# A hybrid attention and mLSTM layer on one core: the mLSTM heads' norm weight applied in ScalarE's copies, and a new order of the three products of a matmul

## The chip, the core and the metric

The kernel runs on one core of one Trainium2 chip. The core has a matrix engine (TensorE, PE in the profile, with its weight loads listed apart as PEld), a vector engine (VectorE, DVE), a scalar engine (ScalarE, ACT), a general engine (GpSimd, POOL) and a queue engine (SyncE, SP) that here only issues DMAs. Each engine runs its own instructions in order; they meet through semaphores. The metric is the device time of one execution in microseconds. Three runs of the kernel before took 2602.81, 2605.07 and 2609.3 us: median 2605.07 us.

## What is computed

One layer of a diffusion backbone over 256 latent tokens and 256 context tokens of width 2048, all in fp32: a half-step SwiGLU feed-forward, a mixer of eight attention heads and eight bidirectional mLSTM heads, and a second feed-forward (latent tokens alone). The change is in the mixer's end and in how every fp32 product is made. Of the reference:

```python
def mixer_output(att, hm, mo, m_gain, w_out):
    B, T = att.shape[:2]
    hm = rms_norm(hm, m_gain.reshape(M_HEADS, HEAD_DIM)) * mo.reshape(B, T, M_HEADS, HEAD_DIM)
    return jnp.concatenate([att.reshape(B, T, ATT_Q_W), hm.reshape(B, T, M_W)], axis=-1) @ w_out
```

`hm` are the mLSTM heads' outputs, `mo` is the sigmoid of a projection, and `m_gain` is the norm's weight: one number for each of the 8 x 128 channels of the heads, the same for all tokens. So it may be multiplied in at any point between the norm and the product with `w_out`.

## The kernel before

**Products in three parts.** An fp32 operand is held as a high part `hi` (rounded to the matrix engine's fp32r type) and a low part `lo`, the rest. A product of two such operands is three matmuls into the same PSUM bank: high by high, high by low and low by high. `mm3` (L147 to L151) makes them. Its arguments are the output, the stationary operand's two parts `sh`, `sl` and the moving operand's two parts `mh`, `ml`. Before, L149 is `sh` by `mh`, L150 is `sh` by `ml`, L151 is `sl` by `mh`. In a profile row of a matmul the name behind the arrow is the moving operand, then the stationary one: `mm<-hi,hhi` moves a weight's high part past an activation's high part.

In most calls the activations stand still and the weights move. In three places the weights stand still: the fourth up-projection tile of both feed-forwards (L764, L1963) and `channels` (L1437), which projects the mLSTM queries and keys.

**Weights.** `load_split` (L140) has SP load a tile of 128 x 2048 fp32 into one of three `raw` buffers. `split` (L119) then makes, for each half of 1024 columns, the high part by a ScalarE copy (L127) and the low part by a VectorE subtraction (L128), each into a ring of four buffers. So the high part of a half is always done first, its low part a copy's and a subtraction's time later; a buffer is free again when the last matmul that reads it is done. The Strassen-like stages of the feed-forwards (`quad`, `pair`) take part of their weights from `chain` and `ra` buffers, to which GpSimd's queue adds further weights by accumulating DMAs (L730). Beside all this, VectorE makes the modulation vectors by long multiply-and-sum instructions (L207), whose rows SP loads (`sraw`, `sr`, `late`).

**The mixer's end.** The heads' outputs lie in `hm`, tokens on partitions. `ev_o` (L1625) evacuates the projection `mo`: a sigmoid on ScalarE into `gm` (L1627), and then a GpSimd product of `gm` with `mg` (L1628), the norm weight broadcast over all partitions by a DMA of SP (L1673). `mlstm_out` (L1719) squares and sums the heads (L1725, L1727), has GpSimd make the reciprocal root (L156, L157), and multiplies `hm` on VectorE by `gm` (L1729) and by the root (L1730). `mlstm_cat` (L1735) turns `hm` with four 128 x 128 transposes into a PSUM bank, channels on partitions, and ScalarE copies the bank to `cx` (L1743), 128 x 512 in one instruction. There are four such copies (two groups of heads, two token tiles). `mlstm_split` then splits `cx` into the `cathi`, `catlo` operand of the output projection `out_proj` (L1804).

In the same stretch runs `attention` (L1676), in steps woven between the projections' matmuls: three products to the scores, the row maximum and its scaling on VectorE (L1686, L1687), the exponential on ScalarE (L1690), the reciprocal sum and a scaling on VectorE (L1691, L1692), transposes on TensorE (L1698), a ScalarE copy (L1700), and the product with the values (L1707).

**What sets the order.** The source gives the order of work by generators that are stepped by hand (`weave`, `steps`). From it the program's builder lays out each engine's instructions, by times it assumes for them; only pinned instructions keep the source's order. So an instruction that costs another time, or depends on another one, can shift others on its engine.

Of the kernel before, what the change touches and what calls it, by code (L numbers as in the profile page):

```python
# [9 lines left out]
F32 = mybir.dt.float32  # L10
# [3 lines left out]
AF = mybir.ActivationFunctionType  # L14
ALU = mybir.AluOpType
# [4 lines left out]
P = 128  # L20
D = 2048
KT = D // P
T = 256
HD = 128
NH = 8
# [33 lines left out]
def tile_layer(ctx: ExitStack, tc: tile.TileContext, I: dict, out: bass.AP):  # L59
    nc = tc.nc  # L60
    pool = lambda **k: tc.tile_pool(**k)

    cst = ctx.enter_context(pool(name="cst", bufs=1))
# [29 lines left out]
    vector, tensor, scalar = [nc.vector], [nc.tensor], [nc.scalar]  # L93
# [12 lines left out]
    triangle(ident, ones, 1)  # L106
    triangle(ident, ident, -1)

    vecs = cst.tile([P, 9 * KT + 3 * KT + 16 * 5 + 16], F32, name="vecs")
    bmT = vecs[:, 0:144].rearrange("p (c k) -> p c k", c=9)  # L110
    gnT = vecs[:, 144:192].rearrange("p (c k) -> p c k", c=3)
    cwT = vecs[:, 192:272].rearrange("p (m j) -> p m j", j=5)
    cbT = vecs[:, 272:288]

    def raw_tile(n=2048):
        t = wp.tile([P, 2048], F32, tag="raw", name="raw", bufs=3)
# [27 lines left out]
        next(beside["load"], None)  # L144
        return wt

    def mm3(out_ap, sh, sl, mh, ml, first, last, skip=False):  # L147

        tensor[0].matmul(out_ap, sh, mh, start=first, stop=False, skip_group_check=skip)  # L149
        tensor[0].matmul(out_ap, sh, ml, start=False, stop=False, skip_group_check=skip)  # L150
        tensor[0].matmul(out_ap, sl, mh, start=False, stop=last, skip_group_check=skip)  # L151

    def rsqrt_mean(ss, n, width=1):

# [35 lines left out]
    nc.scalar.activation(cc, cc, AF.Silu)  # L190
    SC = cst.tile([P, 3, 2, KT], F32, name="SC")
    SH = cst.tile([P, 3, 2, KT], F32, name="SH")
    cst.tile([P, 48], F32, name="cstpad")
    mod_rows = {i: dr.tile([2, D], F32, name=f"mod{i}") for i in (2, 5, 8)}
    mT = cst.tile([P, 9, 2, KT, 2], F32, name="mT")

# [69 lines left out]
    class Beside:  # L266
# [26 lines left out]
        def one(self):  # L293
            i, kt, h = self.items[self.n]
            x, limit = self.slots[self.n]
            mod_half(x, {LAT: self.cB}, None, i, (LAT,), kt, h)
            self.due.append((self.done + 1, self.n))
            self.n += 1
# [158 lines left out]
    hhi = hpool.tile([P, KT, 512], F32R, tag="hh", name="hhi")  # L457
    hlo = hpool.tile([P, KT, 512], F32R, tag="hl", name="hlo")

    pre = [[bank(), bank()] for _ in range(NPRE)]  # L460
    with pool(name="st", bufs=1) as st:
# [61 lines left out]
        rest = []  # L523
# [102 lines left out]
        for n, (s, t) in enumerate(((CTX, 1), (LAT, 0), (LAT, 1))):  # L626
# [5 lines left out]
            last, r = r, factor(ss)  # L632
# [14 lines left out]
        for k0, k1 in BLOCKS[1:]:  # L647
# [26 lines left out]
            if k1 - k0 == 1:  # L674
                tb = tbank()
# [55 lines left out]
    with pool(name="f1u", bufs=1) as f1u:  # L731
# [26 lines left out]
        for f in range(NPRE, FB):  # L758
            pab = []
            for ab in range(2):  # L760
                wt = load_split(I["w_up1"][f - NPRE, ab])
                b = bank()
                for k in range(KT):
                    mm3(b, *wt(slice(k * P, (k + 1) * P)), hhi[:, k, :], hlo[:, k, :], k == 0, k == KT - 1)  # L764
                pab.append(b)
            tail(f, pab)

# [405 lines left out]
    hhi = hpool.tile([P, KT, 512], F32R, tag="hh", name="hhi")  # L1173
    hlo = hpool.tile([P, KT, 512], F32R, tag="hl", name="hlo")
# [79 lines left out]
    with ExitStack() as mx:  # L1254
# [144 lines left out]
        C1 = one([P, NH, 2, 130], "C1")  # L1399
# [32 lines left out]
        def channels(name, h, N, b):  # L1432

            wt = load_split(I[name][h])
            for k in range(KT):
                w = slice(k * P, (k + 1) * P)
                mm3(b, *wt(w), hhi[:, k, 512 - N :], hlo[:, k, 512 - N :], k == 0, k == KT - 1)  # L1437
                if k % 4 == 3:
                    next(beside["part"], None)
                    yield  # L1440
# [11 lines left out]
        for h in range(NH):  # L1452
            b = bank()
# [171 lines left out]
        def ev_o(c, t, b):  # L1625
            o = gm[:, t - 2, c * 512 : (c + 1) * 512]
            nc.scalar.activation(o, b, AF.Sigmoid)  # L1627
            nc.gpsimd.tensor_tensor(o, o, mg[:, c * 512 : (c + 1) * 512], op=ALU.mult)  # L1628

        av = one([P, 4, 256], "av", tag="slot0")  # L1630

# [37 lines left out]
            nc.scalar.activation(k1[:, x], keys[1][x].bitcast(F32), AF.Copy)  # L1669
        keys[1] = [k1[:, x] for x in range(2)]  # L1670
        gm = one([P, 2, 1024], "gm", tag="mkT")
        mg = one([P, 1024], "mg", tag="C1")
        nc.sync.dma_start(mg, I["m_gain"].partition_broadcast(P))  # L1673
        catf = one([P, NH, T], "catf", tag="v1l")

        def attention(kv):  # L1676
# [56 lines left out]
        cxs = {}  # L1733

        def mlstm_cat(c):  # L1735

            for t in range(2):
                tb = tbank()
                for g in range(4):
                    o = (4 * c + g) * P  # L1740
                    nc.tensor.transpose(tb[:, g * P : (g + 1) * P], hm[:, t, o : o + P], ident)
                cxs[c, t] = m1.tile([P, 512], F32, tag="nM", name="cx")
                nc.scalar.activation(cxs[c, t], tb, AF.Copy)  # L1743
                yield

        bo = ({}, {})
# [181 lines left out]
    with f2x:  # L1928
# [28 lines left out]
        for f in range(NPRE, FB):  # L1957
            pab = []
            for ab in range(2):
                wt = load_split(I["w_up2"][f - NPRE, ab])  # L1960
                b = (tbank() if f == FB - 1 else bank())[:, :T]
                for k in range(KT):
                    mm3(b, *wt(slice(k * P, (k + 1) * P)), h2hi[:, k, :T], h2lo[:, k, :T], k == 0, k == KT - 1)  # L1963
                pab.append(b)
            sa = sab_tile()[:, :T]
            nc.scalar.activation(sa, pab[0], AF.Silu)
            gated = nc.vector.tensor_tensor(sa, sa, pab[1], op=ALU.mult)
            split_hid(hids[0], f, sa)
# [379 lines left out]
def _laid_out(a):  # L2348
    asc = np.ascontiguousarray
    part = lambda v: v.reshape(-1, P).T  # L2350
    m = {
        "x": asc(a["x"][0]),
        "ctx": asc(a["ctx"][0]),
        "cc": asc(np.concatenate([a["c_ctx"].reshape(KT, P), a["c"].reshape(KT, P)])),
        "b_mod": asc(a["b_mod"][0].reshape(9, D)),
        "gate_b": asc(a["gate_b"][0]),
        "m_gain": asc(a["m_gain"][0]),
        "q_gain": asc(a["q_gain"][0]),
        "k_gain": asc(a["k_gain"][0]),
        "g_final": asc(a["g_final"]),  # L2360
        "rope": _rope_tables(),
    }
    cw = a["conv_w"][0].T.reshape(16, P, 5).transpose(1, 0, 2).reshape(P, 80)
    m["vecs"] = asc(np.concatenate([part(a["b_mod"][0]), part(a["g_norm"][0]), cw, part(a["conv_b"][0])], 1))

    wm = a["w_mod"][0].reshape(D, 9, D)

    def units(i, a_, b):
        n = (b - a_) * P
        k = 2048 // n  # L2370
        return wm[:, i, a_ * P : b * P].reshape(KT // k, k, P, n).transpose(0, 2, 1, 3).reshape(KT // k, P, 2048)

    def block(k0, k1):

        still = [wm[:, 0, k0 * P : (k0 + 1) * P].T[None]] if k1 - k0 == 2 else []
        return still + [units(0, k1 - 1, k1), units(1, k0, k1)]

    m["w_m0"] = asc(np.concatenate([u for b in BLOCKS for u in block(*b)]))
    m["w_mt"] = asc(wm[:, 2:].reshape(D, 7, KT, P).transpose(1, 2, 3, 0))
    for n in "12":  # L2380
        up, dn = a[f"w_ffn{n}_up"][0], a[f"w_ffn{n}_down"][0]
        nf = dn.shape[0] // P
        up = up.reshape(KT, P, 2, nf, P)

        rest = up[:, :, :, FB:].reshape(4, 4, P, 2, nf // FB - 1, CB)
        m[f"w_up{n}b"] = asc(rest.transpose(4, 3, 0, 2, 1, 5).reshape(nf // FB - 1, 2, 4, P, 2048))
        first = up[:, :, :, :FB].transpose(3, 2, 1, 0, 4).reshape(-1, 2, P, 2048)
        m[f"w_up{n}"] = asc(first[NPRE:])
        pre = first[:NPRE].reshape(2 * NPRE, P, KT, P)
        loads = []  # L2390
        for k0, k1 in BLOCKS if n == "1" else BLOCKS2:
            most = min(2 * NPRE, 2048 // ((k1 - k0) * P) // 2 * 2)
            loads += [pre[u : u + most, :, k0:k1].transpose(1, 0, 2, 3).ravel() for u in range(0, 2 * NPRE, most)]
        m[f"w_pre{n}"] = asc(np.concatenate(loads))
        m[f"w_dn{n}"] = asc(dn.reshape(NF // FB, FB, P, NCB, CB).transpose(0, 3, 2, 1, 4).reshape(NF // FB, NCB, P, 2048))
    w = a["w_in"][0]

    def tokens_still(cols):
        n = cols.shape[1]
        return asc(cols.reshape(4, 4, P, n).transpose(0, 2, 1, 3).reshape(4, P, 4 * n))  # L2400

    def tokens_move(c0):
        return asc(w[:, c0 : c0 + 1024].reshape(KT, P, NH, P).transpose(2, 1, 0, 3).reshape(NH, P, 2048))

    m["w_a"] = tokens_still(np.concatenate([w[:, GT0:], w[:, MV0 : MV0 + 384]], 1))
    m["w_b"] = tokens_still(w[:, MV0 + 384 : MV0 + 768])
    m["w_c"] = asc(w[:, MV0 + 768 : MV0 + 1024].reshape(2, 8, P, 256).transpose(0, 2, 1, 3).reshape(2, P, 2048))
    m["w_mk"], m["w_mq"] = tokens_move(MK0), tokens_move(MQ0)
    m["w_kv"] = tokens_still(w[:, AK0 : AK0 + 512])
    for c in range(2):  # L2410
        m[f"w_q{c}"] = tokens_still(w[:, AQ0 + 512 * c : AQ0 + 512 * (c + 1)])
        m[f"w_o{c}"] = tokens_still(w[:, MO0 + 512 * c : MO0 + 512 * (c + 1)])
    m["w_out"] = asc(a["w_out"][0].reshape(4, 4, P, NCB, CB).transpose(3, 0, 2, 1, 4).reshape(NCB, 4, P, 2048))
    return m
# [15 lines left out]
```

## Time and profile before

| | |
|---|---|
| median of three runs | 2605.07 us |
| profiled execution, its own time | 2604.58 us |
| its span, first to last instruction | 2602.7 us |
| mean granted TensorE clock | 0.996 |
| VectorE busy | 2170.6 us (83%) |
| ScalarE busy | 1417.7 us (54%) |
| GpSimd busy | 220.7 us (8%) |

The profile is one execution: the page sums up engines, queues and the costliest groups of instructions; other views list instructions in order of time, who waited for whom, and the busy time of each engine in a given stretch. A row of an instruction in order of time has its start, its duration (both us), its engine and line, and in brackets how long its engine had been idle and what released it. Matmul durations overlap: a matmul starts before the one before it has drained, so what counts is the distance from start to start. By stage: the first 130 us are the start-up, the first feed-forward lasts to about 1340 us, the mixer to about 1900 us, the second feed-forward to the end.

### The profile page before, as it was taken

Reading aid. Unit: us, or ns where it says so; the run is one execution under the profiler, and the core shown is the slowest. Engines: PE = TensorE matmul, PEld = TensorE weight load, DVE = VectorE, ACT = ScalarE, POOL = GpSimd, SP = SyncE. Lnnn points to the kernel's source line nnn. Section 1 sums busy time; section 2 is a strip of 40 time slices with the busy share of each in tenths; the row PEclk is TensorE's granted clock in tenths of the full one; section 3 lists DMA queues with packets and bytes.
Section 4 is the critical chain, followed back from the end, with each engine's and each line's share of the span. In section 5 each row is a group of like instructions: output and inputs, shape, how many; then the busy total and the mean of one; then the engine's idle time right before and its main releaser. Section 6 shows DMA issues by size and latency. Waiting matters only on the chain.

```text
span 2602.7 us, 33781 instructions
## 1 busy us (share of the span) xinstructions
PE 2575.7 (99%) x12670; PEld 2144.7 (82%) x12670; DVE 2170.6 (83%) x2864; ACT 1417.7 (54%) x1810; POOL 220.7 (8%) x269
## 2 busy tenths in 40 slices
PE   8999999999999999999999999999999999999998
PEld 5788888888888888888889889888897888888887
DVE  7788888878888788888887889798889878887887
ACT  4454444544444565444454347456476676666664
POOL 0000000100000100000110000120000000000001
PEclk8999999999999999999999999999999999999999
DMA  9889999999999988889987887776768988999876
GB/s 392 350 217 265 276 277 271 262 273 285 261 287 265 278 247 240 218 215 228 225 253 266 296 312 247 242 273 213 267 239 240 269 269 260 272 273 279 256 231 176
DMA packets 127219, 681.01 MB, mean 262 GB/s; under 512 B 14152, under 2 KB 16712, under 8 KB 64976
## 3 DMA queue, kind: packets, MB, share of 16 engines
q1 hardware_dynamic: 98544, 493.25, 50.7%
q0 software_dynamic: 28512, 185.61, 36.4%
q8 instruction: 99, 1.62, 0.2%
q14 instruction: 64, 0.52, 0.1%
HBM read 660.91 MB, written 17.89 MB: 261 GB/s over the span
## 4 chain that ended last, share of the span: by engine, by line
PE 85%; DVE 7%; DMA 5%; issue 2%; ACT 1%; POOL 0%; ACTq 0%; POOLq 0%; SPq 0%; DVEq 0%
PE mm L151 21%; PE mm L150 21%; PE mm L149 21%; DVE lo L128 2%; PE mm L87 2%; PE Y L149 2%; PE Y L151 2%; PE Y L150 2%; PE X L151 2%; PE X L150 2%; PE X L149 2%; PE tr L150 1%; PE tr L149 1%; PE tr L151 1%; PE tr L87 1%
## 5 line engine op out<-in xcount | busy, mean ns | idle before, releaser
L127 ACT ACTIVATE hi<-raw 128x1024 fp32r<-128x1024 f32 (+2 forms) x500 | 517.8, 1041 | 421.1 <-PE mm L151 264.1
L128 DVE TENSOR_TENSOR lo<-raw,hi 128x1024 fp32r<-128x1024 f32 (+2 forms) x488 | 583.6, 1207 | 149.7 <-ACT hi L127 130.5
L127 ACT ACTIVATE hi<-chain 128x1024 fp32r<-128x1024 f32 x336 | 355.0, 1059 | 305.7 <-PE mm L151 188.0
L128 DVE TENSOR_TENSOR lo<-chain,hi 128x1024 fp32r<-128x1024 f32 x336 | 407.2, 1221 | 118.0 <-ACT hi L127 114.3
L149 PE MATMUL mm<-hi,hhi 128*128 128x512 f32 (+3 forms) x1024 | 393.6, 385 | 0.0
L151 PE MATMUL mm<-hi,hlo 128*128 128x512 f32 (+3 forms) x1024 | 386.7, 378 | 0.0
L150 PE MATMUL mm<-lo,hhi 128*128 128x512 f32 (+3 forms) x1024 | 386.7, 378 | 0.0
L207 DVE SCALAR_TENSOR_TENSOR junk<-sraw,cBh 128x1024 fp8e5<-128x1024 f32 x192 | 234.3, 1220 | 19.2 <-DMA sraw<-in_w_mt 16.7
L151 PEld LDWEIGHTS mm<-hi,hlo 128*128 128x128 f32 x1024 | 192.5, 188 | 33.9
L149 PEld LDWEIGHTS mm<-hi,hhi 128*128 128x128 f32 x1024 | 192.6, 188 | 31.0
L150 PEld LDWEIGHTS mm<-lo,hhi 128*128 128x128 f32 x1024 | 192.8, 188 | 30.7
L128 DVE TENSOR_TENSOR lo<-ra,hi 128x1024 fp32r<-128x1024 f32 x96 | 117.0, 1223 | 39.7 <-ACT hi L127 35.8
L127 ACT ACTIVATE hi<-ra 128x1024 fp32r<-128x1024 f32 x96 | 101.9, 1061 | 65.1 <-PE mm L151 48.4
L149 PE MATMUL mm<-hi,hid2h 128*128 128x512 f32 x352 | 137.1, 390 | 0.0
L151 PE MATMUL mm<-hi,hid2l 128*128 128x512 f32 x352 | 137.0, 389 | 0.0
L150 PE MATMUL mm<-lo,hid2h 128*128 128x512 f32 x352 | 136.9, 389 | 0.0
L207 DVE SCALAR_TENSOR_TENSOR sr<-sr,cBl 128x1024 f32<-128x1024 f32 x84 | 103.0, 1234 | 14.7 <-DMA sr<-in_w_mt 13.8
L730 POOL DMA_DIRECT2D chain<-in_w_up1b x60 | 53.1, 886 | 726.0 <-DVE lo L128 648.9
L149 PE MATMUL mm<-hhi,hi 128*128 128x512 f32 (+1 forms) x288 | 101.4, 352 | 0.0
L151 PE MATMUL mm<-hhi,lo 128*128 128x512 f32 (+1 forms) x288 | 99.0, 344 | 0.0
L150 PE MATMUL mm<-hlo,hi 128*128 128x512 f32 (+1 forms) x288 | 98.7, 343 | 0.0
L149 PE MATMUL mm<-hi,sumshl 128*128 128x512 f32 x200 | 77.8, 389 | 0.0
(517 smaller groups left out, 5650.3 us busy)
## 6 DMA issues: line engine op xcount, KB each, us to landing
raw<-in_w_dn SPq DMA_DIRECT2D x70, 1024.0 KB, 7.5
chain<-in_w_up1b POOLq DMA_DIRECT2D x60, 1024.0 KB, 9.8
sraw<-in_w_mt SPq DMA_DIRECT2D x96, 512.0 KB, 7.8
sr<-in_w_mt SPq DMA_DIRECT2D x81, 512.0 KB, 5.5
raw<-in_w_up1b SPq DMA_DIRECT2D x40, 1024.0 KB, 7.9
mraw<-in_w_m SPq DMA_DIRECT2D x32, 1024.0 KB, 7.4
raw<-in_w_up2b SPq DMA_DIRECT2D x32, 1024.0 KB, 9.9
chain<-in_w_dn POOLq DMA_DIRECT2D x30, 1024.0 KB, 8.6
```

Of the source, the lines that this page charges most:

```text
L87: ins = getattr(self.engine, name)(*a, **k)
L127: scalar[0].activation(hi, src, AF.Copy)
L128: vector[0].tensor_tensor(lo, src, hi.bitcast(F32), op=ALU.subtract)
L149: tensor[0].matmul(out_ap, sh, mh, start=first, stop=False, skip_group_check=skip)
L150: tensor[0].matmul(out_ap, sh, ml, start=False, stop=False, skip_group_check=skip)
L151: tensor[0].matmul(out_ap, sl, mh, start=False, stop=last, skip_group_check=skip)
L207: ins = nc.vector.scalar_tensor_tensor(junk() if junk else raw, raw, 1.0, cB[s], op0=ALU.mult, op1=ALU.mult, accum_out=mT[:, i, s, kt, h : ...
L730: accum = lambda dst, src: nc.gpsimd.dma_start(dst, src, accum_op=ALU.add)
```

## The change

Three parts.

1. `vecs`, the tile of small vectors loaded at the start, grows by 8 columns, `mgT`, which hold the norm weight with channels on partitions. A pad (`cstpad`) shrinks by 8 columns, so that what lies behind it stays where it was. The load of `mg` and its tile are gone.
2. The four GpSimd products with `mg` are gone. The four ScalarE copies of 128 x 512 to `cx` become sixteen copies of 128 x 128, one for each head and token tile, each with that head's column of `mgT` as its scale for each partition.
3. `mm3` now makes `sh` by `mh`, then `sl` by `mh`, then `sh` by `ml`. Calls where the weights stand still pass `still=True` and keep the old order, so that in every call with weights the weights' low part is read last.

```diff
-    vecs = cst.tile([P, 9 * KT + 3 * KT + 16 * 5 + 16], F32, name="vecs")
+    vecs = cst.tile([P, 9 * KT + 3 * KT + 16 * 5 + 16 + NH], F32, name="vecs")
+    mgT = vecs[:, 288:296]
...
-    def mm3(out_ap, sh, sl, mh, ml, first, last, skip=False):
-
-        tensor[0].matmul(out_ap, sh, mh, start=first, stop=False, skip_group_check=skip)
-        tensor[0].matmul(out_ap, sh, ml, start=False, stop=False, skip_group_check=skip)
-        tensor[0].matmul(out_ap, sl, mh, start=False, stop=last, skip_group_check=skip)
+    def mm3(out_ap, sh, sl, mh, ml, first, last, skip=False, still=False):
+
+        rest = ((sh, ml), (sl, mh)) if still else ((sl, mh), (sh, ml))
+        for n, (s, m) in enumerate(((sh, mh), *rest)):
+            tensor[0].matmul(out_ap, s, m, start=first and not n, stop=last and n == 2, skip_group_check=skip)
...
-    cst.tile([P, 48], F32, name="cstpad")
+    cst.tile([P, 40], F32, name="cstpad")
...
             nc.scalar.activation(o, b, AF.Sigmoid)
-            nc.gpsimd.tensor_tensor(o, o, mg[:, c * 512 : (c + 1) * 512], op=ALU.mult)
...
-        mg = one([P, 1024], "mg", tag="C1")
-        nc.sync.dma_start(mg, I["m_gain"].partition_broadcast(P))
...
-                nc.scalar.activation(cxs[c, t], tb, AF.Copy)
+                for g in range(4):
+                    w = slice(g * P, (g + 1) * P)
+                    nc.scalar.activation(cxs[c, t][:, w], tb[:, w], AF.Copy, scale=mgT[:, 4 * c + g : 4 * c + g + 1])
```

The calls at L764, L1437 and L1963 get `still=True`, and the host's layout of the inputs puts the norm weight into `vecs`.

More of the change, by code (lines that the diff above doesn't have):

```diff
@@ L763, in tile_layer @@
                 for k in range(KT):
-                    mm3(b, *wt(slice(k * P, (k + 1) * P)), hhi[:, k, :], hlo[:, k, :], k == 0, k == KT - 1)
+                    mm3(b, *wt(slice(k * P, (k + 1) * P)), hhi[:, k, :], hlo[:, k, :], k == 0, k == KT - 1, still=True)
                 pab.append(b)
@@ L1436, in channels @@
                 w = slice(k * P, (k + 1) * P)
-                mm3(b, *wt(w), hhi[:, k, 512 - N :], hlo[:, k, 512 - N :], k == 0, k == KT - 1)
+                mm3(b, *wt(w), hhi[:, k, 512 - N :], hlo[:, k, 512 - N :], k == 0, k == KT - 1, still=True)
                 if k % 4 == 3:
@@ L1962, in tile_layer @@
                 for k in range(KT):
-                    mm3(b, *wt(slice(k * P, (k + 1) * P)), h2hi[:, k, :T], h2lo[:, k, :T], k == 0, k == KT - 1)
+                    mm3(b, *wt(slice(k * P, (k + 1) * P)), h2hi[:, k, :T], h2lo[:, k, :T], k == 0, k == KT - 1, still=True)
                 pab.append(b)
@@ L2356, in _laid_out @@
         "gate_b": asc(a["gate_b"][0]),
-        "m_gain": asc(a["m_gain"][0]),
         "q_gain": asc(a["q_gain"][0]),
@@ L2363, in _laid_out @@
     cw = a["conv_w"][0].T.reshape(16, P, 5).transpose(1, 0, 2).reshape(P, 80)
-    m["vecs"] = asc(np.concatenate([part(a["b_mod"][0]), part(a["g_norm"][0]), cw, part(a["conv_b"][0])], 1))
+    m["vecs"] = asc(np.concatenate([part(a["b_mod"][0]), part(a["g_norm"][0]), cw, part(a["conv_b"][0]), part(a["m_gain"][0])], 1))
     wm = a["w_mod"][0].reshape(D, 9, D)
```

## The prediction

> **What bounds the kernel now.** I read the page's shares first, then the chain of waits, then the wait list of TensorE, then stretches of the time line. The page:
>
> ```profile
> span 2602.7 us, 33781 instructions
> PE 2575.7 (99%) x12670; PEld 2144.7 (82%) x12670; DVE 2170.6 (83%) x2864; ACT 1417.7 (54%) x1810; POOL 220.7 (8%) x269
> PE 85%; DVE 7%; DMA 5%; issue 2%; ACT 1%; POOL 0%; ACTq 0%; POOLq 0%; SPq 0%; DVEq 0%
> PE mm L151 21%; PE mm L150 21%; PE mm L149 21%; DVE lo L128 2%; PE mm L87 2%; PE Y L149 2%; PE Y L151 2%; PE Y L150 2%; PE X L151 2%; PE X L150 2%; PE X L149 2%; PE tr L150 1%; PE tr L149 1%; PE tr L151 1%; PE tr L87 1%
> ```
>
> TensorE is busy all but 27 us of the span, and the three lines of `mm3` are the chain. So a gain has to come either from the distance at which matmuls follow each other, or from TensorE's idle time. The idle time by stretch (stretch, its length, then busy us of PE, PEld, DVE, ACT and POOL with their instructions):
>
> ```profile
> 0.00:130.00 130.00, 120.08 (x961) 82.54 (x962) 97.69 (x185) 58.55 (x116) 4.18 (x13) 0.95 0.93 371
> 130.00:1480.00 1350.00, 1348.43 (x6231) 1130.36 (x6230) 1124.21 (x1412) 666.66 (x777) 125.76 (x150) 1.00 0.92 256
> 1480.00:1680.00 200.00, 199.32 (x1118) 173.84 (x1117) 170.61 (x327) 112.95 (x214) 12.92 (x18) 1.00 0.79 273
> 1680.00:1840.00 160.00, 156.10 (x825) 130.30 (x824) 139.99 (x261) 93.80 (x148) 26.35 (x26) 1.00 0.72 249
> 2500.00:2602.70 102.70, 93.36 (x419) 76.85 (x418) 76.62 (x93) 47.11 (x58) 8.08 (x10) 0.97 0.66 201
> ```
>
> Start-up idles 9.9 us; its products are not made by `mm3`. The last stretch idles 9.3 us, nearly all behind the last matmul. What lies between is 27.0 - 9.9 - 9.3 = 7.8 us, and 3.9 of it falls into 1680 to 1840 us, where the heads' norm weight is applied. All that the change can win by ending waits is these 7.8 us.
>
> **Part 1, the order of the products.** What TensorE waited for, and what the makers of the parts waited for (who, for whom: us in total, times, longest):
>
> ```profile
> ACT hi L127 <- PE mm L151: 500.6, 408, 5.3
> DVE lo L128 <- ACT hi L127: 280.7, 250, 4.3
> PE Y L150 <- DVE lo L128: 0.3, 1, 0.3
> PE mm L150 <- DVE lo L128: 0.3, 1, 0.3
> ```
>
> TensorE waits 0.6 us in all for a low part that moves (L150). The new order asks for that part one product later, so at most 0.6 us goes; the makers wait for TensorE and not the reverse. The other side: where the *activation's* low part is the late one, the new order asks for it a product earlier. That is so at the first products of the output projection:
>
> ```profile
> 1791.53 0.45 PE L149 MATMUL mm<-hi,cathi 128*128 128x512 f32 x1
> 1791.82 0.39 PE L150 MATMUL mm<-lo,cathi 128*128 128x512 f32 x1
> 1791.96 0.19 PEld L151 LDWEIGHTS mm<-hi,catlo 128*128 128x128 f32 x1 [0.18 <-DVE catlo L1800]
> ```
>
> L150 of this group now stands behind the wait for `catlo`: so the wait hides one product less: 0.29 us from L149's start to L150's, for each of two token tiles, 0 to +0.6 us; I take +0.3. Against that I take -0.3 of the 0.6. Part 1 sums to 0, between -0.6 and +0.6.
>
> That leaves the matmuls' distance. In the middle of the first feed-forward:
>
> ```profile
> 600.39 0.39 PE L149 MATMUL mm<-hi,s2h 128*128 128x512 f32 x1
> 600.62 0.39 PE L150 MATMUL mm<-lo,s2h 128*128 128x512 f32 x1
> 600.85 0.39 PE L151 MATMUL mm<-hi,s2l 128*128 128x512 f32 x1
> 601.08 0.39 PE L149 MATMUL mm<-hi,s2h 128*128 128x512 f32 x1
> ...
> L150 PEld LDWEIGHTS mm<-lo,hhi 128*128 128x128 f32 x1024 | 192.8, 188 | 30.7
> L151 PEld LDWEIGHTS mm<-hi,hlo 128*128 128x128 f32 x1024 | 192.5, 188 | 33.9
> ```
>
> Each starts 0.23 us after the one before, whether the stationary part is the same as before (L149 to L150) or another. A weight load of 188 ns runs under every matmul: 12670 loads for 12670 matmuls on the page. So giving up the shared stationary part costs nothing. The Trainium skill's page "TensorE: Matmul & The Clock Gate" (section "Step-by-step: what each phase is for") speaks against the change: loading is a separate instruction so that one can load once and multiply repeatedly, and the new order never uses a stationary part twice in a row. By that rule the change adds a load to each group, and is slower; by the rows no load is saved before, so none is added. It is a rival below.
>
> **Part 2, the GpSimd products.** In the mixer's end, in order of time:
>
> ```profile
> 1728.95 2.13 POOL L1628 TENSOR_TENSOR gm<-gm,mg 128x512 f32<-128x512 f32 x1
> 1729.85 2.31 DVE L207 SCALAR_TENSOR_TENSOR sr<-sr,cBl 128x1024 f32<-128x1024 f32 x1
> 1735.62 1.30 POOL L1628 TENSOR_TENSOR gm<-gm,mg 128x512 f32<-128x512 f32 x1
> 1736.95 0.69 DVE L1729 TENSOR_TENSOR hm<-hm,gm 128x512 f32<-128x512 f32 x1 [2.38 <-POOL gm L1628]
> 1740.32 0.39 PE L151 MATMUL mm<-hhi,hlo 128*128 128x512 f32 x1
> 1743.23 0.68 DVE L1686 TENSOR_REDUCE nm<-mm 128x1 f32<-128x512 f32 x1
> 1743.83 1.21 DVE L207 SCALAR_TENSOR_TENSOR sr<-sr,cBl 128x1024 f32<-128x1024 f32 x1
> 1747.50 0.49 DVE L1692 TENSOR_SCALAR pr<-pr,sd 128x512 f32<-128x512 f32 x1
> 1748.13 0.63 PE L1698 MATMUL tr<-ident,pr 128*128 128x128 f32 x4 [2.14 <-DVE pr L1692]
> 1760.60 0.69 DVE L1729 TENSOR_TENSOR hm<-hm,gm 128x512 f32<-128x512 f32 x1 [2.61 <-POOL gm L1628]
> ```
>
> VectorE idles 2.38 us for a GpSimd product, and one of its long instructions takes 2.31 us beside the other product against 1.21 a little later: 3.5 us lost before 1737 us. The scores of an attention step are there at 1740.32 + 0.39 = 1740.7, but VectorE reaches their maximum only at 1743.23, 2.5 us late, with earlier work in front. From there the step runs to `pr` at 1747.50, and TensorE stands 2.14 us at its transposes. Without the products `hm` by `gm` waits for the sigmoid alone, VectorE is 3.5 us ahead, the maximum starts when the scores are there, and the 2.5 us saved cover the 2.14. So -2.1 us. Bounds: 0, if other work of VectorE fills the time, and -3.9, all the idle time of the stretch. I take -2.1, the row that names the wait. The second wait, of 2.61, freed too, has no stall of TensorE behind it. What is late next is the load copies of ScalarE, which wait for TensorE anyway.
>
> The load of `mg` goes too. SP stood before it, and a weight load stood behind:
>
> ```profile
> SPq L1673 <- PE tr L1525: 2.9, 1, 2.9
> 1707.03 0.33 SPq L1673 DMA_DIRECT2D mg<-in_m_gain x1
> 1711.44 0.33 SPq L142 DMA_DIRECT2D raw<-in_w_o  x1
> ```
>
> The next issue came 4.4 us after it, so it had a wait of its own: nothing. Eight more columns in 288 of the first load: nothing.
>
> **Part 3, sixteen copies for four.** ScalarE copies with a scale of 128 x 128 from PSUM already exist, and, from SBUF, two in a row of that size:
>
> ```profile
> 1658.42 0.68 ACT L1491 ACTIVATE A<-nM,hcb 128x128 f32<-128x128 f32 x2
> 1702.90 0.37 ACT L1532 ACTIVATE hm<-tr,den 128x128 f32<-128x128 f32 x1 [1.37 <-DVE den L1530]
> 1779.09 0.60 ACT L1743 ACTIVATE cx<-tr 128x512 f32<-128x512 f32 x1 [0.38 <-PE tr L1741]
> 1780.55 1.06 ACT L127 ACTIVATE hi<-raw 128x1024 fp32r<-128x1024 f32 x1 [0.85 <-PE mm L151]
> 1797.79 1.06 ACT L127 ACTIVATE hi<-raw 128x1024 fp32r<-128x1024 f32 x1 [0.25 <-PE mm L151]
> ```
>
> Two take 0.68, one 0.37: each further one 0.31. Four take 0.37 + 3 x 0.31 = 1.30, against 0.60: +0.7 each, +2.8 in all. The first has 0.85 us of idle behind it. The last two stand in a stretch where ScalarE has 0.25 us to spare; 2 x 0.7 - 0.25 = +1.2 us if TensorE needed the next weights at once. I take 0: their buffers hold two tiles, and TensorE waits 0.6 us for parts in the whole run. Without that cover it is the 1.2.
>
> **The sum** against the profiled execution (2604.58, of which 2602.7 is span): 0 - 2.1 + 0 gives 2602.5 us. That execution lies 0.5 below the median of the runs, which cover 2602.8 to 2609.3. By the bounds: -0.6 - 3.9 = -4.5 to +0.6 + 1.2 = +1.8, so 2600.1 to 2606.4, and with the runs' own spread of some 3 us either way 2597 to 2609.
>
> **Rivals.**
>
> *Every wait in the middle goes* (faster). Earlier high parts and a freer VectorE end all 7.8 us of idle: 2596.8. For it: half lies where the products go. Against it: the rest is scattered among causes the change leaves alone.
>
> *The attention steps slip* (slower). Between 1740 and 1840 us TensorE comes to sixteen attention steps in order, each with a chain through VectorE, ScalarE, VectorE that nothing else covers. The builder lays the engines' work out anew; if in five of them a ScalarE copy or a modulation product (1.21) comes in front of the exponential or the scaling, each costs what the one slip in the profile costs, 2.14: +10.7, 2615.3. It decides from four slips on. For it: VectorE is 140.0 of 160 us busy there, and a slip exists already. Against it: GpSimd's products, in that one's past, are gone.
>
> *The low part's buffer* (slower). It is now read by the last product, so it comes free 0.23 us later. Where VectorE waits for that buffer and not for the high part, each half is late by it; 46 halves make 10.6 us, 2615.2. It decides from 36 halves on (8.3 us). Against it: the low part's rows wait for the high part (280.7 us), whose copy takes 1.06 us first.
>
> *The shared stationary part was worth something* (slower). The loads of L151, a fresh part, stand 33.9 us idle in 1024, those of L150, the repeated one, 30.7. With 63% of the span in `mm`, 1640 us at 3 x 0.23 a group, there are 2380 groups: 2.3 x 3.2 = +7.4, 2612.0. It is the mechanism of the Trainium skill's rule above.
>
> **How the numbers follow.** Forecast 0.58; every wait gone 0.13; slipped steps 0.17; buffer 0.09; stationary 0.03. The predicted time is the forecast's, 2602.5; its own range is 2597 to 2609. Faster or slower counts from 0.3%, about what a measurement of this kernel can tell from no change: below 2597.3 or above 2612.9. Faster: 0.13 + 0.02 of the forecast's edge = 0.15. Slower: 0.17 + 0.09 + 0.01 of the stationary part's, which lies just below the bound, = 0.27. The same: 0.56 + 0.02 = 0.58. The range runs from 2596, which takes in the faster rival, to 2616, which takes in the slower ones as priced; some 0.15 lies outside, where more steps slip.
>
> **What would show it.** The distance of matmuls stays 0.23 us. The brackets at L1729 name ScalarE, the transposes' 2.14 us are gone, the sixteen copies take about 0.3 us each, and the idle time of 1680 to 1840 us is near 1.8. Wrong: another distance, or idle time of TensorE in the feed-forwards.

## The result, and the profile after

The changed kernel takes 2601.22 us (median of 11 runs, 2599.06 to 2603.37); the kernel before, in 11 runs beside it, 2605.10 us (2602.81 to 2613.92). The ratio is 0.998, with a 95% interval of 0.9971 to 0.9989: 2.9 to 7.6 us faster. The forecast was 2602.5 us, a gain of 2.1 us against the profiled execution; the gain is clear of the noise and about twice that size.

The profiled execution of the changed kernel took 2600.28 us, 4.3 us less than that of before. First the page: span and busy times. The matmuls of `mm3` are now all on one line, L152.

```profile
span 2598.0 us, 34128 instructions
PE 2574.4 (99%) x12670; PEld 2145.3 (83%) x12670; DVE 2172.5 (84%) x2864; ACT 1419.1 (55%) x1822; POOL 216.1 (8%) x265
```

The work is the same: 12670 matmuls and 12670 loads, VectorE's 2864 instructions; twelve more on ScalarE, four fewer on GpSimd. TensorE's idle time fell from 27.0 to 2598.0 - 2574.4 = 23.6 us, and the rest of the difference in span, 1.3 us, is busy time (2575.7 to 2574.4). The same stretches as before (stretch, length, busy us of PE, PEld, DVE, ACT and POOL):

```profile
0.00:130.00 130.00, 119.32 (x958) 81.86 (x959) 96.94 (x184) 58.62 (x116) 4.17 (x13) 0.95 0.93 369
130.00:1480.00 1350.00, 1349.37 (x6237) 1131.68 (x6236) 1127.20 (x1415) 667.10 (x777) 125.37 (x150) 1.00 0.93 257
...
1680.00:1840.00 160.00, 158.72 (x836) 132.57 (x835) 141.03 (x263) 96.78 (x160) 22.85 (x22) 1.00 0.72 252
...
2500.00:2598.00 98.00, 88.57 (x399) 72.91 (x397) 72.96 (x89) 45.30 (x57) 8.07 (x10) 0.98 0.64 198
```

Idle time of TensorE is a stretch's length less its busy time. In the mixer's end (1680 to 1840 us) it fell from 3.9 to 1.3 us, which is where the prediction looked for the gain. Start-up is 0.8 us worse, the stretch from 130 to 1480 us (the first feed-forward and the beginning of the mixer) 0.9 us better (1.57 to 0.63); whether that is the change or one execution against another is a question for the experiments.

The instructions in order of time, changed kernel, where the products with `mg` stood:

```profile
1728.42 0.69 DVE L1727 TENSOR_TENSOR hm<-hm,gm 128x512 f32<-128x512 f32 x1
1730.15 1.22 DVE L208 SCALAR_TENSOR_TENSOR sr<-sr,cBl 128x1024 f32<-128x1024 f32 x1
1734.98 0.69 DVE L1727 TENSOR_TENSOR hm<-hm,gm 128x512 f32<-128x512 f32 x1
1739.96 0.40 PE L152 MATMUL mm<-hlo,hhi 128*128 128x512 f32 x1
1741.56 0.69 DVE L1684 TENSOR_REDUCE nm<-mm 128x1 f32<-128x512 f32 x1
1744.69 0.49 DVE L1690 TENSOR_SCALAR pr<-pr,sd 128x512 f32<-128x512 f32 x1
1745.45 0.60 PE L1696 MATMUL tr<-ident,pr 128*128 128x128 f32 x4
1756.14 0.69 DVE L1727 TENSOR_TENSOR hm<-hm,gm 128x512 f32<-128x512 f32 x1 [1.23 <-ACT gm L1628]
```

`hm` by `gm` has no bracket at 1728.42 and at 1734.98: the second of the two waits for nothing where VectorE had idled 2.38 us. The long modulation product takes 1.22 us, not 2.31. The row maximum comes at 1741.56, still 1.2 us after the scores (1739.96 + 0.40), where it was 2.5 us. `pr` is ready at 1744.69 + 0.49 = 1745.2, against 1748.0 before, and the transposes at 1745.45 start without the 2.14 us wait. The one wait left at L1727 names ScalarE's sigmoid.

The copies, in order of time and as a tile (durations are min/median/max ns; then who waited for `cx`):

```profile
1776.15 1.14 ACT L1743 ACTIVATE cx<-tr,vecs 128x128 f32<-128x128 f32 x4 [0.75 <-PE tr L1739]
1784.24 1.13 ACT L1743 ACTIVATE cx<-tr,vecs 128x128 f32<-128x128 f32 x4
1790.42 2.17 ACT L1743 ACTIVATE cx<-tr,vecs 128x128 f32<-128x128 f32 x8
...
L1743 ACT ACTIVATE cx<-tr,vecs x16: 357/376/422, 1776.2 to 1792.2; 128x128 f32<-128x128 f32 x16
  PEld mm L152: 0.9, 3
  PE mm L152: 0.2, 1
```

Four copies take 1.14 us where one took 0.60: +0.54 each, about +2.2 in all.

What TensorE still waited for on these two accounts (us in total, times, longest):

```profile
PE mm L152 <- DVE lo L129: 0.4, 2, 0.2
PE Y L152 <- DVE lo L129: 0.3, 1, 0.3
...
PE tr L1696 <- DVE pr L1690: 0.3, 1, 0.3
```

Low parts of weights 0.7 us, against 0.6 before, so this list shows no gain from the new order; the transposes 0.3 us.

### The profile page after: what moved, and what is told of

Same layout as the page of the kernel before. It is cut to its first block, busy times and chain, and to the rows that moved or that the text cites. A ratio compares the mean times of both kernels' runs of the same rounds, so it can differ in the third digit from the quotient of the medians.

```text
span 2598.0 us, 34128 instructions
## 1 busy us (share of the span) xinstructions
PE 2574.4 (99%) x12670; PEld 2145.3 (83%) x12670; DVE 2172.5 (84%) x2864; ACT 1419.1 (55%) x1822; POOL 216.1 (8%) x265
## 5 line engine op out<-in xcount | busy, mean ns | idle before, releaser
L152 PE MATMUL mm<-hi,hhi 128*128 128x512 f32 (+3 forms) x1024 | 394.0, 385 | 0.0
L152 PE MATMUL mm<-lo,hhi 128*128 128x512 f32 (+3 forms) x1024 | 387.0, 378 | 0.2 <-DVE lo L129 0.2
L152 PE MATMUL mm<-hi,hlo 128*128 128x512 f32 (+3 forms) x1024 | 386.4, 377 | 0.0
L152 PEld LDWEIGHTS mm<-lo,hhi 128*128 128x128 f32 x1024 | 192.5, 188 | 34.5 <-DVE lo L129 0.6
L152 PEld LDWEIGHTS mm<-hi,hhi 128*128 128x128 f32 x1024 | 192.6, 188 | 31.0
L152 PEld LDWEIGHTS mm<-hi,hlo 128*128 128x128 f32 x1024 | 192.8, 188 | 30.7
L152 PE MATMUL mm<-lo,hid2h 128*128 128x512 f32 x352 | 137.1, 389 | 0.0
L152 PE MATMUL mm<-hi,hid2h 128*128 128x512 f32 x352 | 137.0, 389 | 0.0
L152 PE MATMUL mm<-hi,hid2l 128*128 128x512 f32 x352 | 136.9, 389 | 0.0
L152 PE MATMUL mm<-hi,sumshl 128*128 128x512 f32 x400 | 123.2, 389 | 0.0
L152 PE MATMUL mm<-hi,sumshh 128*128 128x512 f32 x352 | 108.4, 389 | 0.0
L152 PE MATMUL mm<-hhi,hi 128*128 128x512 f32 (+1 forms) x288 | 101.4, 352 | 0.0
L152 PE MATMUL mm<-hhi,lo 128*128 128x512 f32 (+1 forms) x288 | 99.0, 344 | 0.0
```

The costliest lines, as they stand in the source:

```text
L152: tensor[0].matmul(out_ap, s, m, start=first and not n, stop=last and n == 2, skip_group_check=skip)
```

## The experiments

The question is which part brought the 4 to 5 us. In the expectations theory A is the one of the prediction: the gain is that of the GpSimd products, the order of the products is worth nothing. Its rival B: the order itself is worth something, because the weights' low part, which is made last, is asked for later. All ratios are against the kernel before, run beside it on the same chip; each variant has 11 runs.

### Each part alone, both, and the order reversed

The order alone; the products, `mg` and the four plain copies as before (only the line with the order is shown):

```diff
+        rest = ((sh, ml), (sl, mh)) if still else ((sl, mh), (sh, ml))
```

> Only the new order of the three products; GpSimd's products and the load of mg are as before. Theory A (the gain comes from GpSimd's products in the mixer's end, the order is worth about nothing): 2604 to 2606 us, ratio to before 0.9995 to 1.0005, TensorE still idles about 3.9 us between 1680 and 1840 us, with the transposes waiting some 2 us for pr. Rival B (the order is worth half or more, since TensorE waits less at the start of the second feed-forward, where 0.8 us less idle stands in the changed kernel's trace): 2602 to 2603 us, ratio about 0.999, and idle time between 1900 and 2000 us falls from 1.6 to about 0.8.

Measured: 2603.48 us, ratio 0.9993 (0.9984 to 1.0001). The chain of the products is as it was. In order of time, and the stretch of the mixer's end:

```profile
1730.80 2.13 POOL L1628 TENSOR_TENSOR gm<-gm,mg 128x512 f32<-128x512 f32 x1
1731.70 2.31 DVE L207 SCALAR_TENSOR_TENSOR sr<-sr,cBl 128x1024 f32<-128x1024 f32 x1
...
1749.18 0.63 PE L1698 MATMUL tr<-ident,pr 128*128 128x128 f32 x4 [2.02 <-DVE pr L1692]
...
1680.00:1840.00 160.00, 155.60 (x821) 129.36 (x819) 139.48 (x261) 93.16 (x149) 26.65 (x26) 1.00 0.72 249
```

The same 2.31, the same wait of 2 us at the transposes, 4.4 us idle in the stretch. So the end of that wait belongs to the products, not to the order. The time is just below theory A's range, and the idle time from 1900 to 2000 us, 1.3 us, lies between the two theories' values.

The products alone; the norm weight in the copies, the three matmuls in the old order (the main lines, against the kernel before):

```diff
+        rest = ((sh, ml), (sl, mh))
...
-            nc.gpsimd.tensor_tensor(o, o, mg[:, c * 512 : (c + 1) * 512], op=ALU.mult)
...
+                    nc.scalar.activation(cxs[c, t][:, w], tb[:, w], AF.Copy, scale=mgT[:, 4 * c + g : 4 * c + g + 1])
```

> Only the norm weight in ScalarE's copies; the products keep the old order. Theory A: the whole gain, 2601 to 2602 us, ratio about 0.998 to 0.9985, idle between 1680 and 1840 us at 1.3 to 1.8 us and no long wait of the transposes for pr. Rival B: about half, 2603 us, ratio 0.999, and 1900 to 2000 us as before.

Measured: 2602.73 us, ratio 0.999 (0.9981 to 0.9999), about 2.6 us. In its trace:

```profile
1680.00:1840.00 160.00, 158.02 (x834) 132.15 (x833) 141.15 (x264) 96.90 (x161) 21.42 (x22) 1.00 0.72 251
```

2.0 us idle, and no wait of the transposes for `pr` is left. The fall from 3.9 to 2.0 us is close to the forecast's -2.1. But the products alone do not bring theory A's "whole gain" of 0.998 to 0.9985: the ratio is the 0.999 of rival B.

Both, which is the changed kernel once more:

> The changed kernel itself, on the same chip as the two halves: ratio 0.998. If the halves add up, the two ratios' distances from 1 sum to this one's.

Measured: 2603.14 us, ratio 0.9986 (0.9977 to 0.9995), about 3.6 us. The sum of the two parts' ratios is 0.9983.

The changed kernel with the moving low part asked for first of three instead of last:

```diff
-        rest = ((sh, ml), (sl, mh)) if still else ((sl, mh), (sh, ml))
-        for n, (s, m) in enumerate(((sh, mh), *rest)):
+        three = ((sh, mh), (sh, ml), (sl, mh)) if still else ((sh, ml), (sh, mh), (sl, mh))
+        for n, (s, m) in enumerate(three):
```

> The changed kernel, but where the weights move their low part is asked for first of the three, two products (0.45 us) earlier than in the changed kernel. Theory A: low parts lie ready well before they are read, so nothing but the places where TensorE waits for them now (0.6 us in all) grows: at most +1 us against the changed kernel, ratio to before 0.998 to 0.9985. Rival B (the slack of the low part is what the order buys): every tile begins up to 0.45 us later wherever the low part is just in time, several us slower, ratio 1.000 or above.

Measured: 2606.0 us, ratio 1.0001 (0.9992 to 1.0011): the gain of the products is gone again, though the products are. Against the changed kernel beside it that is 2.9 us by the medians, more than A allowed. Its waits of TensorE for low parts (us in total, times, longest), and below them those of the second profile of the changed kernel:

```profile
PE tr L152 <- DVE lo L129: 1.7, 1, 1.7
PE Y L152 <- DVE lo L129: 0.5, 2, 0.3
PE mm L152 <- DVE lo L129: 0.4, 1, 0.4
```

```profile
PE tr L152 <- DVE lo L129: 1.9, 1, 1.9
PE mm L152 <- DVE lo L129: 0.4, 1, 0.4
PE Y L152 <- DVE lo L129: 0.3, 1, 0.3
```

Both hold one long wait for a low part, of 1.7 and 1.9 us. The second list is the changed kernel itself, whose first profile has no such wait: it comes and goes between executions of one kernel. The traces so do not show where the order's time lies.

### The copies, the products' dose, the shared stationary part

The changed kernel with four plain copies and the norm weight applied nowhere:

```diff
-                for g in range(4):
-                    w = slice(g * P, (g + 1) * P)
-                    nc.scalar.activation(cxs[c, t][:, w], tb[:, w], AF.Copy, scale=mgT[:, 4 * c + g : 4 * c + g + 1])
+                nc.scalar.activation(cxs[c, t], tb, AF.Copy)
```

> The changed kernel with the four plain copies of 128x512 back in place of the sixteen; the heads' norm weight is applied nowhere. It prices the sixteen copies alone. Theory A (ScalarE's 0.55 us more in each of four places is hidden): same as the changed kernel within 0.5 us, ratio to before 0.998 to 0.9987. Rival (they stand in front of the split of the output projection's first operand, where TensorE waits some 0.9 us in the changed kernel): 1 us faster than the changed kernel, and these waits shrink to about 0.2.

Measured: 2600.11 us, ratio 0.9983 (0.9974 to 0.9992): the changed kernel's, inside the intervals, which are too wide (2.3 us either way) to settle the expected half microsecond. The tile of the copies, as above:

```profile
L1741 ACT ACTIVATE cx<-tr x4: 587/596/602, 1777.6 to 1792.4; 128x512 f32<-128x512 f32 x4
  PEld mm L152: 0.9, 3
  PE mm L152: 0.2, 1
```

Behind the copies TensorE's matmuls waited 0.2 us and its weight loads 0.9 us, with four copies as with sixteen. The rival asked for the 0.9 to shrink, and it did not: by these waits the 2.2 us of ScalarE lie beside other work.

The kernel before with each GpSimd product made twice, so that the norm weight enters squared:

```diff
             nc.gpsimd.tensor_tensor(o, o, mg[:, c * 512 : (c + 1) * 512], op=ALU.mult)
+            nc.gpsimd.tensor_tensor(o, o, mg[:, c * 512 : (c + 1) * 512], op=ALU.mult)
```

> The kernel before with each GpSimd product made twice, so the norm weight is in the output squared; eight products for four. Theory A (TensorE waits at the second step's transposes because VectorE stands behind the products): that wait grows from 2.1 us by the two or three products in its past, 1.3 to 2.1 us each, to 5 us or more; 2608 to 2611 us, ratio 1.001 to 1.002. Rival (products are beside the path, the gain was a new layout of the work): ratio 1.000 and the wait stays near 2.

Measured: 2611.53 us, ratio 1.0021 (1.0012 to 1.003), +5.5 us. In order of time, and the stretch:

```profile
1729.29 3.26 POOL L1628 TENSOR_TENSOR gm<-gm,mg 128x512 f32<-128x512 f32 x1
1730.17 1.23 DVE L207 SCALAR_TENSOR_TENSOR sr<-sr,cBl 128x1024 f32<-128x1024 f32 x1
...
1740.06 0.69 DVE L1730 TENSOR_TENSOR hm<-hm,gm 128x512 f32<-128x512 f32 x1 [4.22 <-POOL gm L1629]
1743.70 0.63 PE L1699 MATMUL tr<-ident,pr 128*128 128x128 f32 x4 [2.67 <-DVE pr L1693]
1751.24 0.63 PE L1699 MATMUL tr<-ident,pr 128*128 128x128 f32 x4 [2.14 <-DVE pr L1693]
1774.09 0.63 PE L1699 MATMUL tr<-ident,pr 128*128 128x128 f32 x4 [1.30 <-DVE pr L1693]
...
1680.00:1840.00 160.00, 152.09 (x795) 126.99 (x793) 137.39 (x255) 90.84 (x143) 31.38 (x30) 0.99 0.67 236
```

VectorE's wait for the product grows from 2.38 to 4.22 us. TensorE's waits for `pr` grow from 2.8 us, in two, to 7.0 us, in four; three are shown, and none reaches the 5 us that theory A expected of a single one. The time lies just above the expected range. The idle time of the stretch doubles, from 3.9 to 7.9 us. With no products, one set and two sets, all in the old order, it is 2.0, 3.9 and 7.9 us in one trace each. The other traces agree: it is 1.2 to 2.8 us in the seven traces without products and 2.9 to 4.4 in the four with one set. This is the prediction's chain (product, VectorE, `pr`, transposes), seen at three doses.

The changed kernel with the low part last, but the two matmuls that share a stationary part side by side:

```diff
+        three = ((sh, mh), (sh, ml), (sl, mh)) if still else ((sl, mh), (sh, mh), (sh, ml))
```

> The changed kernel, with the three products where the weights move in the order low standing by high, high standing by high, high standing by low: the weights' low part is still last, and the two products with the same standing part are again neighbours. Theory A: matmuls follow each other at 0.227 us whatever stands, so the same as the changed kernel, ratio 0.998 to 0.9987. Rival (the shared standing part is worth something, and the change gave it away): faster than the changed kernel by 2 to 7 us, ratio 0.996 to 0.9975, and a start-to-start distance below 0.227 us within the pair.

Measured: 2602.02 us, ratio 0.9982 (0.9973 to 0.9991): the changed kernel's time. The loads of this kernel's groups (busy us, mean ns | idle before), in the order in which they run second, third, first:

```profile
L152 PEld LDWEIGHTS mm<-hi,hhi 128*128 128x128 f32 x1024 | 192.8, 188 | 30.7
L152 PEld LDWEIGHTS mm<-lo,hhi 128*128 128x128 f32 x1024 | 192.5, 188 | 34.4 <-DVE lo L129 0.5
L152 PEld LDWEIGHTS mm<-hi,hlo 128*128 128x128 f32 x1024 | 192.7, 188 | 31.0
```

The prediction's rival read 33.9 us of idle time before a fresh stationary part and 30.7 before a repeated one as its price. Here the third load repeats the second's stationary part and idles 34.4, of which 0.5 is a wait for a low part. The 3 us belong to the third place of a group, not to the freshness of the part: the rival falls by its own row. The order asks for the activation's low part first, and at the output projection that may have a price: one new wait in the order of time, for which the trace names no releaser:

```profile
1793.71 0.47 PE L152 MATMUL mm<-hi,catlo 128*128 128x512 f32 x1 [1.19 <-issue]
1794.02 0.39 PE L152 MATMUL mm<-hi,cathi 128*128 128x512 f32 x1
1794.25 0.40 PE L152 MATMUL mm<-lo,cathi 128*128 128x512 f32 x1
```

The last two rows are a pair with one stationary part, and their starts are 0.23 us apart. The changed kernel asks for `catlo` second, one product later, and its traces have no such wait.

The kernel before without the products and without `mg`, four plain copies, the old order, so the norm weight applied nowhere:

```diff
-            nc.gpsimd.tensor_tensor(o, o, mg[:, c * 512 : (c + 1) * 512], op=ALU.mult)
-        mg = one([P, 1024], "mg", tag="C1")
-        nc.sync.dma_start(mg, I["m_gain"].partition_broadcast(P))
```

> The kernel before with the four GpSimd products and the load of mg taken out and nothing in their place; the norm weight is applied nowhere, the copies are the four of before, the order of the products is the old one. Theory A: the wait of 2.1 us at the transposes is gone, ratio 0.999, 2.0 to 3.0 us faster than before and equal to the kernel with the norm weight in ScalarE's copies alone. Rival (the gain was the load of mg or the copies' new places): the wait stays, ratio 1.000.

Measured: 2603.09 us, ratio 0.9989 (0.998 to 0.9998), the value of the products alone a second time, now without any change of the copies. From 1680 to 1840 us TensorE idles 2.2 us, and its one wait for `pr` is 0.7 us. One of its stretches and one of its waits show how far single executions go apart:

```profile
130.00:1480.00 1350.00, 1346.18 (x6220) 1128.38 (x6220) 1121.59 (x1409) 665.20 (x775) 125.47 (x150) 1.00 0.92 256
...
PE tr L829 <- DVE ca L842: 3.4, 3, 2.3
```

Up to 1480 us its source is that of before, and it idles 3.8 us there where the profile of before idles 1.6; 3.4 us are waits for `ca`, a product of VectorE in the first feed-forward. The changed kernel itself idles 0.6 us there in one profile and 2.9 us in the other. A gain of 1 or 2 us spread over the feed-forwards cannot be read from one trace.

### The order's worth, once more

What stayed open was the order: worth nothing, or 1 to 2 us. The kernel before with the low part first of three, and the order alone again (the edit shown is the first one's):

```diff
+        three = ((sh, mh), (sh, ml), (sl, mh)) if still else ((sh, ml), (sh, mh), (sl, mh))
```

> The kernel before, GpSimd's products kept; where weights are the moving operand the product with their low part stands first of three, one product (0.23 us) earlier than before. Theory S (the low part's lead is short, and each product by which it is asked for later is worth 1 to 2 us in all, because a part is late now and then in every execution): 1 to 3 us slower than before, ratio 1.0004 to 1.0012, and in the waits of TensorE more time than 0.6 us put down to VectorE's low parts. Theory N (the order is worth nothing; the 1.8 us of the order alone was the spread of the runs): ratio within 0.0003 of 1.

> The order of the changed kernel alone, products kept, a second time with more rounds, beside the kernel before on the same chip. Theory S: 1 to 2 us faster than before, ratio 0.9992 to 0.9996, with the upper end of the interval below 1. Theory N: ratio within 0.0003 of 1, interval around 1.

Measured: low part first 2606.12 us, ratio 1.0003 (0.9994 to 1.0012); low part last 2602.29 us, ratio 0.9995 (0.9986 to 1.0004). Each interval holds 1, so neither run decides for itself. The waits for low parts with the low part first are 0.9 us, against 0.6 before. All comparisons of the place of the low part, by ratio to the kernel before:

| place of the weights' low part | products kept | products gone |
|---|---|---|
| first | 1.0003 | 1.0001 |
| second (as before) | 1 | 0.999, 0.9989 |
| third (as changed) | 0.9993, 0.9995 | 0.998, 0.9986, 0.9983, 0.9982 |

Both columns fall from row to row. With the products kept the third place gives 0.9994 on average, and if the two runs are taken as independent, half an interval of 0.0009 / 1.41 = 0.0006 on either side: 0.9988 to 1.0000, that is 0 to 3.1 us, 1.6 in the middle. With the products gone (two kernels of the four and one of the two at the second place differ by the copies or by the pairing) it is 0.9983 against 0.999: 0.0007, 1.8 us. The expectation that the order alone would show an upper end below 1 was missed. So no comparison of the order alone shows its worth. One pair of variants does differ clearly, the low part first against last with the products gone (1.0001 and 0.9986): 0.0015, with 0.0013 on either side by the same reckoning.

All runs together show it. Each of the 219 timed runs has a place of the low part (first, second, third), a number of products (none, one set, two) and a chip on which it ran. A least-squares fit with one step for the place, one value for each set of products and one level for each chip (the first comparison counted as one of its own) gives -1.65 us for each place later (95% interval -2.2 to -1.1) and +2.5 us for the products (1.7 to 3.2). The runs of one kernel scatter by 2.3 us (standard deviation), and the variants lie about the fit no farther than that lets expect. With any one variant left out, the step stays between -1.2 and -1.9 us. The fit was made after the runs were seen, and it takes them as independent.

## Why the prediction was right, and what it missed

**The products (forecast -2.1): right, by the mechanism and in size.** The products alone gave 0.999 and 0.9989, on average 2.7 us. The chain is shown by its parts. In the four traces with one set of products VectorE waits 1.5 to 2.4 us for one before 1742 us, and in three of them the long modulation product beside the first one takes 2.31 to 2.33 us; without products no trace has either. TensorE's waits for `pr` are 2.0 to 3.5 us in these four traces, 0 to 1.5 in the seven without products, and 7.0 with the products doubled. The row that named the wait was the right value to take from a bound of 0 to -3.9. One link was weaker than foreseen: in the changed kernel the row maximum does not start when the scores are there, but 1.2 us later, and the 1.3 us gained there were enough.

**The copies (forecast +0.7 each, hidden): right.** They take +0.54 each, and TensorE's waits behind `cx` are the same with four as with sixteen.

**The order (forecast 0, between -0.6 and +0.6): this is the term that was mis-sized.** It measures about -1.6 us. The two runs of the order alone leave 0 to -3.1 us open, which reaches into the bounds; the fit over all runs, -2.2 to -1.1, lies outside them. The step that failed reads: "TensorE waits 0.6 us in all for a low part that moves (L150) ... so at most 0.6 us goes". The row was right for its execution, but it was one execution, and the time is that of many: other executions of these kernels hold a single wait of 1.4 to 1.9 us for a low part. A bound from the waits of one trace is a sample and not an upper end. What the order saves, and where, is still open: the totals of TensorE's waits for low parts in single traces (0.3 to 0.9 us in nine of the twelve, 1.7 to 2.6 in three) do not follow the order, and that late low parts are what it saves is not shown. In the other half of the step, the earlier need of `catlo`, its load waits 0.26 us in the changed kernel, against 0.18 before.

**The distance of the matmuls (0.23 us): right.** In the middle of an attention step of the changed kernel:

```profile
1743.41 0.39 PE L152 MATMUL mm<-hi,hhi 128*128 128x512 f32 x1
1743.63 0.39 PE L152 MATMUL mm<-hi,hlo 128*128 128x512 f32 x1
1743.86 0.39 PE L152 MATMUL mm<-lo,hhi 128*128 128x512 f32 x1
```

No stationary part is shared by neighbours any more, and the starts are 0.22 and 0.23 us apart. The Trainium skill's rule that the prediction weighed (the page "TensorE: Matmul & The Clock Gate", section "Step-by-step: what each phase is for") has no price here: each matmul of this kernel has its load, repeated stationary part or not.

**The rivals.** No slower one came: the attention steps did not slip (1.2 to 2.8 us idle in the traces without products, where 10.7 more would have been), the low part's buffer held a product longer cost nothing (the order alone is not slower), the stationary part is worth nothing. "Every wait goes" did not come either: 23.6 us of TensorE's 27.0 idle remain, 20.1 of them at start-up and in the last stretch.

The forecast's sum, 0 - 2.1 + 0, becomes -1.6 - 2.7 + 0 = -4.3 us by the runs of the parts, and the whole change measures -5.2 (-7.6 to -2.9) and, in the second comparison, -3.6 us (-6.0 to -1.3). That the time came within the range is owed in part to the width of the range, which allowed 3 us for the spread of the runs: of the gain only the products' share was foreseen, and the order's came on top.

## What to carry to other kernels

When an engine off the critical path makes a small product, look at who stands behind it in order: here four GpSimd instructions of 1.3 to 2.1 us cost 2.7 us because VectorE waited for one, ran slower beside another, and TensorE's transposes stood behind VectorE. A wait list of one execution bounds what a change can win in that execution; for a part that is late only now and then, compare many runs, or move the suspected cost both ways (earlier, later), see whether the times fall in order, and fit all runs together: here no comparison of the order alone was clear of its interval, and 219 runs were. Multiplying by a weight that is constant per partition costs little where a copy has to be made anyway: sixteen scaled copies in place of four plain ones added 2.2 us of ScalarE's work and no time that the runs could tell.

## What the hardware showed that was not expected

GpSimd and VectorE slow each other, and which one pays changes. In the profile of before, a GpSimd product took 2.13 us, and the VectorE instruction beside its later part 2.31 in place of 1.22. With the products doubled, the first product took 3.26 us; the first long VectorE instruction that started beside it took 1.23 (both rows stand above), and the next one took 2.29:

```profile
1731.34 2.29 DVE L128 TENSOR_TENSOR lo<-raw,hi 128x1024 fp32r<-128x1024 f32 x1
```

The small reciprocal-root instructions pay too, with the products (1.88 us at 1732.30 in the profile of before) and without them. In the changed kernel:

```profile
1728.27 1.01 POOL L158 TENSOR_TENSOR rstd<-rstd,mhalf 128x4 f32<-128x4 f32 x1
1730.37 1.87 POOL L158 TENSOR_TENSOR rstd<-rstd,mhalf 128x4 f32<-128x4 f32 x1
1737.05 2.26 POOL L158 TENSOR_TENSOR rstd<-rstd,mhalf 128x4 f32<-128x4 f32 x1
```

The same operation on 128 x 4 numbers takes 1.01 us here beside a VectorE instruction of 0.69 (L1727 at 1728.42, shown above), as it does while VectorE idles (1.01 at 1734.65 in the profile of before), and 1.87 and 2.26 us beside longer ones. What decides who waits was not tried.
